# A two-block transformer in fp32 on one core: every small product widened to 128 contraction rows, and the states of the gated linear attention made for two chunks at a time

## The chip, the cores and the metric

The program runs on one core of one Trainium2 chip. The metric is the device time of one execution in microseconds, the median of three runs. The trace comes from one more execution, taken by the hardware profiler. TensorE (PE in the rows) does the matrix products, VectorE (DVE) and ScalarE (ACT) work on rows of 128 partitions, GpSimd (POOL) does memsets and a few additions, SyncE (SP) issues the transfers. An operand of TensorE has its contraction along the partitions: a product over 64 rows uses 64 partitions of both operands.

## The reference

512 tokens and 16 meta tokens (528 rows, 1024 features). Block 1 has two layers, each with two mixers side by side, an output projection and a convolutional feed-forward part. Block 2 has an attention in which each query sees the 256 or fewer keys that an index score picks, a short convolution, gates and a gated feed-forward part. What the change touches, cut short:

```python
# gated linear attention: 4 heads, dk 64, dv 128; chunk 0 = the 16 meta tokens, then 8 chunks of 64
u = einsum('bhntk,bhntv->bhnkv', k * exp(log_end - log_b), v)     # one state increment a chunk
S[c] = decay[c][..., None] * S[c-1] + u[c]                         # S[0] = the meta tokens' increment
o = einsum('bhntk,bhnkv->bhntv', q, S)                             # each token reads its chunk's state
# forgetting attention (FoX): 8 heads of 64, query blocks of 128
logits = einsum('bqhd,bkhd->bhqk', q, k) + c_q[..., None] - c_k;  p = softmax(where(causal, logits, -inf));  o = p @ v
# index scores of block 2: 8 heads of 64
rel = relu(einsum('bthd,bsd->bths', q_idx, k_idx));  score = einsum('bths,bth->bts', rel, w_idx)
# its attention: 8 heads of 128 over the chosen keys
```

## The kernel before

**Jobs.** Nearly all of the time goes to products of the activations with weights. A job is one block of 128 weight columns (`steps`, L291): for each 128 rows of the contraction it runs three passes, high part of the weights with the high and the low part of the activations, and low part with high (names wh and wl, L309). 528 tokens are two pieces of 264 columns, 512 without the meta tokens one piece of 512 or, in block 2, two of 258. A step of a job is thus four matmuls with wh and two with wl. Weights arrive by transfers issued ahead; ScalarE and VectorE split them into wh and wl two jobs ahead (L260, L261).

**Side work.** Everything else (gates, scores, softmax, transposes, values, states, norms) is pushed as small functions onto `self.queue` and taken off between a job's steps, `rate` functions a step (`pump`, L286). Attention units go through `push_unit`, stage by stage, each stage one unit later than the one before it: scores, then transposes of the probabilities, then values. The tile framework's list scheduler sets the final order on each engine from these calls; each engine then runs its list in order.

**PSUM.** Three pools of two tiles: "mm" for the jobs, "PS" (`self.PS`, used by scores, index scores, gates, spreads, states and outputs) and "PT" (`self.PT`, for transposes, values and norms). A tile is free again when its last reader is done.

**Products over fewer than 128 rows.** `stacked_scores` (L494) puts the high and the low part of a head's queries (64 features each) into the two row halves, and multiplies them by the key's high part, which stands in both halves (L497, 128 rows); the low part of the keys is multiplied by the high part of the queries alone (L498, 64 rows). FoX and the index scores use it; a FoX score ends with a product that adds the causal mask (L558, bf16), except in the first of the last block's two pieces. The 16 meta keys' values are products over 16 rows (L608 in FoX, as the first two of each group of values; L1120 for block 2, as the last of each block; L574 for the meta queries). `gla_states` (L686) makes a chunk's state increment from 64 tokens, for both heads of a pair, and chains it on VectorE:

```python
            nc.tensor.matmul(ps[:, 128 * b:128 * b + 128], lhsT=st["kt"][m][R0:R0 + 64, C],
                             rhs=st["gvt"][2 * m + b][R0:R0 + 64, C], start=True, stop=True)
...
            nc.vector.scalar_tensor_tensor(dst[R, :], z["cur"][R, :], st["dec"][m][R, c:c + 1],
                                           ps[R, 128 * b:128 * b + 128], op0=ALU.mult, op1=ALU.add)
```

One queued function is one chunk, so nine (`first` for the meta tokens, eight steps) for each of two pairs of heads in each layer. `gla_out` (L739) reads the states per chunk by products of 64 rows onto 64 tokens (L760), four in each of its two halves for each head. `spread` (L201), the gate products (L391), the 16x16 transposes of the meta queries (L568) and the last transposes of each mixer are small as well.

Of the kernel before, what the change touches and what calls it, by code (L numbers as in the profile page):

```python
# [36 lines left out]
class Net:  # L37
# [43 lines left out]
    # ---------------------------------------------------------------- constants  # L81
    def constants(self):
# [26 lines left out]
        self.wa = c.tile([16, 2, 256], F32, name="wa")  # L109
# [48 lines left out]
    # ---------------------------------------------------------------- small helpers  # L158
# [17 lines left out]
    def hs_of(self, src, gain, lo, t0=0, t1=L, hi=None):  # L176
        """hi and lo parts of src * gain over columns t0:t1."""
# [15 lines left out]
    def token_sums(self, acc):  # L193
        """Per-token sums over the features: [128, 5], one column a token block."""
# [6 lines left out]
    def spread(self, r):  # L201
        """[128, L] tile with r's per-token values in every partition."""
# [18 lines left out]
    def norm_at(self, first, sums, spread):  # L221
        """A phase's norm factors, made while its first two jobs run: sums late in the first, spread in the second."""
# [4 lines left out]
    # ---------------------------------------------------------------- weight jobs  # L227
# [17 lines left out]
    def split(self, jb, pin=False):  # L245
        """High and low parts of a job's weights; a packed job has both in one tile, 64 columns each."""
# [20 lines left out]
    def push_unit(self, stages):  # L267
        """Stages of one unit of side work; each stage goes one unit later than the stage before it."""
# [22 lines left out]
    def steps(self, jb):  # L291
        """One job's matrix products, a step for each 128 rows of the weights, then its evacuation."""
# [31 lines left out]
    def run(self, look=2, ahead=4):  # L324
        """The jobs in order; the first two go together, as their operand comes in bit by bit."""
# [25 lines left out]
    def v(t, toks):  # L351
        """View of a [128, L] tile that matches psv of the same tokens."""
# [8 lines left out]
    def scaled(self, ps, toks, rs, out=None, extra=None):  # L361
        """ps * rs (* extra) over the tokens, into a slot."""
# [8 lines left out]
    # ---------------------------------------------------------------- block 1 mixers  # L371
# [1262 lines left out]
```

## Time and profile before

| | before |
|---|---|
| three runs | 2447.89, 2444.22, 2442.56 us |
| median | 2444.22 us |
| span of the profiled execution | 2443.0 us |
| TensorE busy | 2411.0 us, 99% |
| VectorE, ScalarE, GpSimd busy | 1372.8 us (56%), 942.0 us (39%), 228.7 us (9%) |
| weight matmuls of L309 | 13720 of 15831 hardware passes |
| mean transfer rate | 81 GB/s |

The span of the profiled execution lies within the runs, so its rows stand for them. The duration that the trace gives for one matmul overlaps with the next one's; the distance from one start to the next is what a matmul takes on the engine, and the timeline's rows give the starts. A plain fp32 product is run as two hardware passes and stands as x2 there; transposes and the split (fp32r) products are one pass each. A shape like 64*128 ahead of the operand is rows times columns of the array.

### The profile page before, as it was taken

The numbers are of one execution on the slowest core, as the hardware profiler recorded it, in microseconds if no ns is written. First come the engines' busy times: TensorE is split into PE (matmuls) and PEld (weight loads), VectorE is DVE, ScalarE is ACT, GpSimd is POOL, SyncE is SP. The second block draws the span as 40 slices with busy tenths as digits, with TensorE's granted clock in tenths as the row PEclk, the third lists the DMA queues.
The fourth block names the chain that finished last, engine by engine and source line by source line (L and its number), as shares of the span: only waits on it lengthen the run. The fifth ranks groups of instructions, "written<-read, shape, count | busy, mean of one in ns | idle before, by whom it ended". The sixth has DMA issues, their size and how long they took to land.

```text
span 2443.0 us, 37854 instructions
## 1 busy us (share of the span) xinstructions
PE 2411.0 (99%) x15831; PEld 2154.9 (88%) x15831; DVE 1372.8 (56%) x2492; ACT 942.0 (39%) x1609; POOL 228.7 (9%) x216
## 2 busy tenths in 40 slices
PE   7999999999999999999999999999999999999998
PEld 6888999999998888999898988888898888888888
DVE  6556656555555666566464664688344544433335
ACT  6553434333345544434232443332233523222225
POOL 1010110000021101200000031110000002101012
PEclk9999999999998999999999999999999999999999
DMA  4211122232331111222323222232221132232233
GB/s 123 57 53 36 53 87 87 91 100 78 100 85 52 49 39 53 70 87 87 104 83 100 81 90 70 70 104 87 87 69 53 56 100 87 88 102 87 95 99 126
DMA packets 217074, 196.79 MB, mean 81 GB/s; under 512 B 8987, under 2 KB 214791, under 8 KB 216903
## 3 DMA queue, kind: packets, MB, share of 16 engines
q1 hardware_dynamic: 216903, 194.37, 25.7%
q8 instruction: 125, 2.05, 0.4%
q14 instruction: 46, 0.38, 0.1%
HBM read 192.26 MB, written 2.10 MB: 80 GB/s over the span
## 4 chain that ended last, share of the span: by engine, by line
PE 67%; ACT 1%; issue 1%; DVE 1%; POOL 0%; DMA 0%; POOLq 0%; ACTq 0%; SPq 0%; DVEq 0%
PE mm L309 59%; PE valuesT L1120 1%; PE foxV L608 1%; PE scoresS L1103 1%; PE foxS L498 1%; PE idx L498 1%; PE gla_statesS L709 0%; PE foxT L588 0%; PE attend_pT L459 0%; PE spreadS L210 0%; ACT wh L260 0%; PE foxS L497 0%; PE idx L497 0%; PE to_tokensT L445 0%; PE foxS L558 0%
## 5 line engine op out<-in xcount | busy, mean ns | idle before, releaser
L309 PE MATMUL mm<-g,wh 128*128 128x264 f32 (+3 forms) x9168 | 1890.1, 316 | 6.8 <-DVE g L365 4.5
L309 PEld LDWEIGHTS mm<-g,wh 128*128 128x128 f32 x9168 | 1389.5, 190 | 124.2 <-issue 9.8
L309 PE MATMUL mm<-g,wl 128*128 128x264 f32 (+3 forms) x4552 | 1161.8, 313 | 0.0
L309 PEld LDWEIGHTS mm<-g,wl 128*128 128x128 f32 x4552 | 751.3, 189 | 51.6 <-issue 0.3
L260 ACT ACTIVATE wh<-raw 128x1024 fp32r<-128x1024 f32 (+1 forms) x369 | 384.6, 1043 | 978.6 <-PE mm L309 831.2
L261 DVE TENSOR_TENSOR wl<-raw,wh 128x1024 fp32r<-128x1024 f32 (+1 forms) x369 | 444.8, 1206 | 83.1 <-ACT wh L260 58.1
L365 DVE TENSOR_TENSOR g<-mm,g 128x528 f32<-128x528 f32 (+2 forms) x228 | 158.6, 696 | 327.5 <-PE mm L309 324.2
L191 POOL TENSOR_TENSOR g<-g,g 128x528 f32<-128x528 f32 (+3 forms) x49 | 71.5, 1470 | 911.8 <-ACT g L190 911.8
L166 DVE TENSOR_TENSOR g<-g,g 128x512 fp32r<-128x512 f32 (+3 forms) x131 | 91.5, 698 | 39.9 <-ACT g L972 29.0
L997 DVE TENSOR_TENSOR g<-mm,g 128x528 f32<-128x528 f32 (+1 forms) x48 | 33.6, 700 | 118.7 <-PE mm L309 118.6
L954 ACT ACTIVATE g<-g,cv 128x528 f32<-128x528 f32 (+1 forms) x88 | 72.1, 820 | 17.6 <-DVE g L365 17.6
L166 DVE TENSOR_TENSOR g<-foxT,g 16x128 fp32r<-16x128 f32 (+2 forms) x160 | 49.8, 335 | 42.9 <-ACT g L593 35.9
L957 DVE SCALAR_TENSOR_TENSOR g<-g,cv,g 128x526 f32<-128x526 f32 (+1 forms) x88 | 66.8, 760 | 3.1
L956 DVE SCALAR_TENSOR_TENSOR g<-g,cv,g 128x527 f32<-128x527 f32 (+1 forms) x88 | 66.3, 753 | 1.8 <-ACT g L954 1.8
L1383 POOL TENSOR_TENSOR g<-g,g 128x512 f32<-128x512 f32 x22 | 38.9, 1767 | 283.1 <-ACT g L1382 283.1
L968 ACT ACTIVATE g<-g 128x528 f32<-128x528 f32 (+1 forms) x44 | 28.1, 639 | 84.0 <-DVE g L957 84.0
L174 POOL TENSOR_TENSOR sm<-sm,mhalf 128x10 f32<-128x10 f32 (+4 forms) x29 | 36.8, 1279 | 192.5 <-DVE sm L173 192.1
L563 ACT ACTIVATE g<-g,sm 128x144 f32<-128x144 f32 (+2 forms) x80 | 41.4, 517 | 21.1 <-DVE sm L559 18.3
L593 ACT ACTIVATE g<-foxT 128x256 fp32r<-128x256 f32 (+1 forms) x96 | 32.8, 342 | 42.8 <-PE foxT L588 36.8
L970 DVE TENSOR_TENSOR g<-g,g 128x528 f32<-128x528 f32 (+1 forms) x44 | 30.8, 701 | 32.3 <-ACT g L968 32.3
L972 ACT ACTIVATE g<-g 128x528 fp32r<-128x528 f32 (+1 forms) x44 | 28.1, 639 | 33.1 <-DVE g L970 33.1
L1414 DVE TENSOR_TENSOR g<-mm,g 128x512 f32<-128x512 f32 x16 | 11.1, 692 | 50.2 <-PE mm L309 50.2
(264 smaller groups left out, 1699.0 us busy)
## 6 DMA issues: line engine op xcount, KB each, us to landing
raw<-in_w_up_dram SPq DMA_DIRECT2D x50, 1024.0 KB
raw<-in_w_in_dram SPq DMA_DIRECT2D x44, 1024.0 KB
raw<-in_w_down_dram SPq DMA_DIRECT2D x28, 896.0 KB
raw<-in_w_in_dram SPq DMA_DIRECT2D x28, 512.0 KB
raw<-in_w_out_dram SPq DMA_DIRECT2D x12, 1024.0 KB
raw<-in_w_down_dram SPq DMA_DIRECT2D x12, 1024.0 KB
raw<-in_w_gate_dram SPq DMA_DIRECT2D x10, 1024.0 KB
raw<-in_w_up_dram SPq DMA_DIRECT2D x10, 512.0 KB
```

The costliest lines, as they stand in the source:

```text
L166: (eng or self.nc.vector).tensor_tensor(out, x, hi.bitcast(F32), op=ALU.subtract)
L191: nc.gpsimd.tensor_tensor(acc[:, t0:t1], tmp[:, t0:t1], acc[:, t0:t1], op=ALU.add)
L260: keep(nc.scalar.activation(hi[:, :K], src, AF.Copy))
L261: keep(nc.vector.tensor_tensor(lo[:, :K], src, hi[:, :K].bitcast(F32), op=ALU.subtract))
L309: nc.tensor.matmul(ps[:, b, :n], lhsT=w[:, k, :], rhs=x[:, t:t + n], start=(ki == 0 and pi == 0), stop=(ki == len(order) - 1 and pi == len ...
L365: self.nc.vector.tensor_tensor(self.v(out, toks), self.psv(ps, toks), self.v(rs, toks), op=ALU.mult)
L498: self.nc.tensor.matmul(ps[:, :n], lhsT=q[R, q0:q0 + 128], rhs=kl[R, a:a + n], start=False, stop=stop)
L563: nc.scalar.activation(P[:qs, :N], P[:qs, :N], AF.Exp, scale=-1.0, bias=m, accum_out=col)
L954: nc.scalar.activation(A[:, lo:], U[:, lo:], AF.Identity, bias=self.vec("cb", 44 * i + t), scale=cw(2))
L956: nc.vector.scalar_tensor_tensor(A[:, s1:], U[:, s1 - 1:L - 1], cw(1), A[:, s1:], op0=ALU.mult, op1=ALU.add)
L957: nc.vector.scalar_tensor_tensor(A[:, s0:], U[:, s0 - 2:L - 2], cw(0), A[:, s0:], op0=ALU.mult, op1=ALU.add)
L1383: nc.gpsimd.tensor_tensor(z[:, META:], z[:, META:], self.rs[:, META:], op=ALU.mult)
```

## The change

Each product over fewer than 128 rows gets 128 rows, the added ones being zero in one operand or both; and the gated linear attention is arranged so that one product covers two chunks.
- `fox_k` makes one tile of low key parts per head, with zeros in the other head's rows; `stacked_scores` uses all rows. The index keys' low part is built the same way.
- The meta values (`fvm`, `fvms`, `dvm`), the meta keys and values of the linear attention (`km`, `gvm`) and the low-rank gate weights (`wa`) become constants of 128 rows that are zeroed once at the start on GpSimd. `sm`, the gates' input, has its upper rows zeroed.
- `attend_p` transposes all of the first 128 columns of the probabilities as its first block and multiplies them with the zero-padded meta values; up to four blocks share a PSUM tile. FoX's meta columns and the tails are transposed 128x128 as well; `spread` uses all rows for the last, short block.
- `gla_k` writes the keys per head with the two chunks of a 128-token block in different columns, zeros elsewhere (a memset, one copy on ScalarE and one on VectorE), so that one product over 128 tokens gives two chunks' increments in the two row halves. `gla_states` has per pair `first` and two functions `head`, each four products into one PSUM tile and then eight chained VectorE operations that alternate between the halves; the decays are made per head (eight activations a layer in place of two).
- `gla_q`, new, spreads each head's queries over the two row halves by chunk (a memset, two copies on ScalarE, one on VectorE), and `gla_out` needs two products for each half.

```diff
-            nc.vector.tensor_scalar(dg[:sz, :sz], self.ident[:sz, :sz], r[:sz, j:j + 1], None, op0=ALU.mult)
+            nc.vector.tensor_scalar(dg[:, :sz], self.ident[:, :sz], r[:, j:j + 1], None, op0=ALU.mult)
             t, o = (tiles[0], b) if b < HALF else (tiles[1], b - HALF)
-            nc.tensor.matmul(t[:, o:o + sz], lhsT=self.ones[:sz, :], rhs=dg[:sz, :sz], start=True, stop=True)
+            nc.tensor.matmul(t[:, o:o + sz], lhsT=self.ones, rhs=dg[:, :sz], start=True, stop=True)
...
-    def attend_p(self, P, j, qs, vt, vm, mcol, vw, vc):
-        nc = self.nc
+    def attend_p(self, P, j, vt, vm):
+        nc = self.nc
+        cols = [0] + [BLK[k][0] for k in range(1, j + 1)]
+        vals = [vm] + [vt[:, 128 * k:128 * k + 128] for k in range(j)]
         blocks = []
-        if j:
+        for x in range(0, j + 1, 4):
+            n = min(4, j + 1 - x)
             pt = self.PT("attend_pT_")
-            for k in range(1, j + 1):
-                b, _ = BLK[k]
-                nc.tensor.transpose(pt[:, 128 * (k - 1):128 * (k - 1) + qs], P[:qs, b:b + 128],
-                                    self.ident[:qs, :qs])
-            PTs = self.G()
-            self.copy("a" if j % 2 else "v", PTs[:, :128 * j], pt[:, :128 * j])
-            for k in range(1, j + 1):
-                blocks.append((PTs[:, 128 * (k - 1):128 * (k - 1) + qs],
-                               vt[:, 128 * (k - 1) + vc:128 * (k - 1) + vc + vw]))
-        pm = self.PT("attend_pT_")
-        nc.tensor.transpose(pm[:META, :qs], P[:qs, :META], self.ident[:qs, :qs])
-        PM = self.M()
-        self.copy("v", PM[:META, :qs], pm[:META, :qs])
-        blocks.append((PM[:META, :qs], vm[:META, mcol:mcol + vw]))
+            for k in range(n):
+                nc.tensor.transpose(pt[:, 128 * k:128 * k + 128], P[:, cols[x + k]:cols[x + k] + 128], self.ident)
+            PTs = self.G() if n > 1 else self.M()
+            self.copy("v" if x or j % 2 else "a", PTs[:, :128 * n], pt[:, :128 * n])
+            blocks += [(PTs[:, 128 * k:128 * k + 128], vals[x + k]) for k in range(n)]
...
-        st["kl"] = kl = self.G(F32R)
+            kh, kl = self.G(F32R), self.G(F32R)
+            nc.gpsimd.memset(kl[O, :].bitcast(F32), 0.0)
...
-        self.nc.tensor.matmul(ps[:, :n], lhsT=q[R, q0:q0 + 128], rhs=kl[R, a:a + n], start=False, stop=stop)
+        self.nc.tensor.matmul(ps[:, :n], lhsT=q[:, q0:q0 + 128], rhs=kl[:, a:a + n], start=False, stop=stop)
...
+        pv = pt.rearrange("p (j b k) -> p j b k", j=4, b=2)
+        for b in range(2):
+            kt = self.G()
+            nc.gpsimd.memset(kt[:, :512], 0.0)
+            kv = kt[:, :512].rearrange("p (j e k) -> p j e k", j=4, e=2)
+            for e in range(2):
+                R = slice(64 * e, 64 * e + 64)
+                self.copy("v" if e else "a", kv[R, :, e, :], pv[R, :, b, :])
...
-        def step(c):
-            def f():
-                R0, C = 64 * (c % 2), slice(128 * (c // 2), 128 * (c // 2) + 128)
-                ps = self.PS("gla_statesS_")
-                for b in range(2):
-                    nc.tensor.matmul(ps[:, 128 * b:128 * b + 128], lhsT=st["kt"][m][R0:R0 + 64, C],
-                                     rhs=st["gvt"][2 * m + b][R0:R0 + 64, C], start=True, stop=True)
-                dst = z["S"][1 + c // 4][:, 128 * (c % 4):128 * (c % 4) + 128]
-                for b in range(2):
-                    R = slice(64 * b, 64 * b + 64)
-                    nc.vector.scalar_tensor_tensor(dst[R, :], z["cur"][R, :], st["dec"][m][R, c:c + 1],
-                                                   ps[R, 128 * b:128 * b + 128], op0=ALU.mult, op1=ALU.add)
-                z["cur"] = dst
-            return f
-        self.push(first, *[step(c) for c in range(8)])
+                S, ps = self.G(), self.PS("gla_statesS_")
+                for j in range(4):
+                    C = slice(128 * j, 128 * j + 128)
+                    nc.tensor.matmul(ps[:, C], lhsT=st["kt"][h][:, C], rhs=st["gvt"][h][:, C], start=True, stop=True)
+                cur = st["S0"][m][64:, 128 * b:128 * b + 128]
+                for c in range(8):
+                    e, C = c % 2, slice(128 * (c // 2), 128 * (c // 2) + 128)
+                    R, Q = slice(64 * e, 64 * e + 64), slice(64 - 64 * e, 128 - 64 * e)
+                    nc.vector.scalar_tensor_tensor(S[R, C], cur, st["dec"][h][Q, c // 2:c // 2 + 1], ps[R, C],
+                                                   op0=ALU.mult, op1=ALU.add)
+                    cur = S[R, C]
+                st["S"][h] = S
+            return f
+        self.push(first, head(0), head(1))
...
+    def gla_q(self, st, m, t):
+        nc = self.nc
+        for b in range(2):
+            B = slice(64 * b, 64 * b + 64)
+            q = self.G()
+            nc.gpsimd.memset(q, 0.0)
+            tv = t[:, META:].rearrange("p (j e t) -> p j e t", j=4, e=2)
+            qv = q[:, META:].rearrange("p (j e t) -> p j e t", j=4, e=2)
+            nc.scalar.activation(qv[:64, :, 0, :], tv[B, :, 0, :], AF.Copy)
+            nc.vector.tensor_copy(qv[64:, :, 1, :], tv[B, :, 1, :])
+            nc.scalar.activation(q[64:, :META], t[B, :META], AF.Copy)
+            st["gq"][2 * m + b] = q
...
-                for c in range(4 * half, 4 * half + 4):
-                    Sc = (SA if c < 4 else SB)[:, 128 * (c % 4):128 * (c % 4) + 128]
-                    t, x, s0 = META + 64 * c, 128 * (c // 2), 64 * (c % 2)
-                    nc.tensor.matmul(ps[s0:s0 + 64, x:x + 128], lhsT=gq[B, t:t + 64], rhs=Sc[B, :],
+                for j in (2 * half, 2 * half + 1):
+                    C = slice(128 * j, 128 * j + 128)
+                    nc.tensor.matmul(ps[:, C], lhsT=gq[:, META + 128 * j:META + 128 * j + 128], rhs=S[:, C],
                                      start=True, stop=True)
```

Where the instructions stand: on TensorE, in the first layer behind the transposes of a pair's keys and values, before (gla_statesS is the PSUM tile of a chunk's increments, mm a job's):

```order
L309 MATMUL mm_2417<-g_205,wl_2066 128x264 x2
L445 MATMUL to_tokensT_2391<-ident,g_2209 128x128 x4
L448 MATMUL to_tokensT_2397<-ident,g_2209 16x128
L709 MATMUL gla_statesS_2438<-g_1734,g_569 128x128
L709 MATMUL gla_statesS_2438<-g_1744,g_569 128x128
L309 MATMUL mm_2417<-g_223,wh_2065 128x264 x2
L309 MATMUL mm_2417<-g_224,wh_2065 128x264 x2
L309 MATMUL mm_2417<-g_223,wl_2066 128x264 x2
L709 MATMUL gla_statesS_2449<-g_1734,g_569 128x128
L709 MATMUL gla_statesS_2449<-g_1744,g_569 128x128
```

and now:

```order
L322 MATMUL mm_2460<-g_226,wl_2106 128x264
L463 MATMUL to_tokensT_2431<-ident,g_2249 128x128 x4
L466 MATMUL to_tokensT_2437<-ident,g_2249 16x128
L322 MATMUL mm_2460<-g_226,wl_2106 128x264
L735 MATMUL gla_statesS_2479<-g_1774,g_602 128x128 x4
L322 MATMUL mm_2460<-g_244,wh_2105 128x264 x2
L322 MATMUL mm_2460<-g_245,wh_2105 128x264 x2
L322 MATMUL mm_2460<-g_244,wl_2106 128x264 x2
L735 MATMUL gla_statesS_2499<-g_1784,g_606 128x128 x4
L322 MATMUL mm_2460<-g_264,wh_2105 128x264 x2
```

Where a chunk's two products stood in every step of the job, a head's four stand together, two heads one step apart, each group in a PSUM tile of its own.

On VectorE the recurrence of the same pair, before (s is the start state, g a slot of states, dec the decays; each row is both heads):

```order
L714 SCALAR_TENSOR_TENSOR g_2430<-s_2424,dec_557,gla_statesS_2438 64x128 x2
L166 TENSOR_TENSOR g_2402<-g_2400,g_2407 64x528
L714 SCALAR_TENSOR_TENSOR g_2430<-g_2430,dec_557,gla_statesS_2449 64x128 x2
L714 SCALAR_TENSOR_TENSOR g_2430<-g_2430,dec_557,gla_statesS_2454 64x128 x2
L714 SCALAR_TENSOR_TENSOR g_2430<-g_2430,dec_557,gla_statesS_2465 64x128 x2
L714 SCALAR_TENSOR_TENSOR g_2431<-g_2430,dec_557,gla_statesS_2476 64x128 x2
```

and now:

```order
L740 SCALAR_TENSOR_TENSOR g_2478<-s_2467,dec_577,gla_statesS_2479 64x128
L740 SCALAR_TENSOR_TENSOR g_2478<-g_2478,dec_577,gla_statesS_2479 64x128
L179 TENSOR_TENSOR g_2449<-g_2440,g_2448 64x528
L740 SCALAR_TENSOR_TENSOR g_2478<-g_2478,dec_577,gla_statesS_2479 64x128
L740 SCALAR_TENSOR_TENSOR g_2498<-s_2467,dec_580,gla_statesS_2499 64x128
L740 SCALAR_TENSOR_TENSOR g_2478<-g_2478,dec_577,gla_statesS_2479 64x128
L740 SCALAR_TENSOR_TENSOR g_2498<-g_2498,dec_580,gla_statesS_2499 64x128
L740 SCALAR_TENSOR_TENSOR g_2478<-g_2478,dec_577,gla_statesS_2479 64x128
```

Each chunk had a PSUM tile of its own, released after two operations; now eight operations read one tile, and the two heads' chains alternate.

On TensorE the first FoX units of the first layer, before (foxS are scores, foxT transposes, foxV values):

```order
L558 MATMUL foxS_855<-maskb,identb 128x16
L309 MATMUL mm_781<-g_269,wh_659 128x264 x2
L309 MATMUL mm_781<-g_270,wh_659 128x264
L568 MATMUL foxT_861<-ident,g_839 16x16
L309 MATMUL mm_781<-g_270,wh_659 128x264
L309 MATMUL mm_781<-g_269,wl_660 128x264 x2
L574 MATMUL foxV_867<-vm_801,md_863 16x64
L497 MATMUL foxS_878<-g_651,g_714 128x256
```

and now:

```order
L570 MATMUL foxS_895<-maskb,identb 128x128
L322 MATMUL mm_824<-g_288,wh_702 128x264 x2
L322 MATMUL mm_824<-g_289,wh_702 128x264 x2
L322 MATMUL mm_824<-g_288,wl_703 128x264
L580 MATMUL foxT_901<-ident,g_879 128x128
L322 MATMUL mm_824<-g_288,wl_703 128x264
L510 MATMUL foxS_918<-g_690,g_757 128x256
L511 MATMUL foxS_918<-g_691,g_757 128x256
L570 LDWEIGHTS identb
L570 MATMUL foxS_918<-maskb,identb 128x128
```

The meta queries' transposes and values keep their place between the weight matmuls, and have 128 rows.

## Rows read from the trace of the kernel before

**Rows 1.** The page's busy times of the engines

```profile
PE 2411.0 (99%) x15831; PEld 2154.9 (88%) x15831; DVE 1372.8 (56%) x2492; ACT 942.0 (39%) x1609; POOL 228.7 (9%) x216
```

**Rows 2.** Mixer stretch: us; busy PE, PEld, DVE, ACT, POOL; clock; DMA share, GB/s

```profile
56.00:292.00 236.00, 235.87 (x1705) 202.63 (x1703) 147.08 (x394) 116.14 (x293) 29.17 (x45) 1.00 0.17 50
```

**Rows 3.** Waits of TensorE: total us, times, longest us

```profile
PE to_tokensT L445 <- DVE g L676: 3.6, 1, 3.6
```

**Rows 4.** Timeline of TensorE, index scores: start us, us, instruction

```profile
1504.90 0.64 PE L309 MATMUL mm<-g,wh 128*128 128x258 f32 x4
1505.38 0.40 PE L309 MATMUL mm<-g,wl 128*128 128x258 f32 x2
1505.62 0.34 PE L497 MATMUL idx<-g,g 128*128 128x400 f32 x1
1505.90 0.44 PE L498 MATMUL idx<-g,g 64*128 64x400 f32 x1
1506.27 0.76 PE L309 MATMUL mm<-g,wh 128*128 128x258 f32 x4
```

**Rows 5.** Timeline of TensorE, attention of block 2

```profile
1781.69 1.05 PE L1120 MATMUL valuesT<-g,g 128*128 128x128 f32 x8
1782.68 0.48 PE L1120 MATMUL valuesT<-md,dvm 16*128 16x128 f32 x2
1783.09 0.75 PE L309 MATMUL mm<-g,wh 128*128 128x264 f32 x4
1783.68 0.40 PE L309 MATMUL mm<-g,wl 128*128 128x264 f32 x2
```

**Rows 6.** Timeline of TensorE, states of the gated linear attention

```profile
195.56 0.41 PE L309 MATMUL mm<-g,wl 128*128 128x264 f32 x2
195.90 0.71 PE L709 MATMUL gla_statesS<-g,g 64*128 64x128 f32 x4
196.54 0.74 PE L309 MATMUL mm<-g,wh 128*128 128x264 f32 x4
```

**Rows 7.** Timeline of TensorE, FoX scores; a 16x16 transpose behind a mask

```profile
79.23 0.28 PE L497 MATMUL foxS<-g,g 128*128 128x256 f32 x1
...
79.75 0.23 PE L558 MATMUL foxS<-maskb,identb 128*128 128x128 bf16 x1
79.79 0.72 PE L309 MATMUL mm<-g,wh 128*128 128x264 f32 x4
80.35 0.41 PE L309 MATMUL mm<-g,wl 128*128 128x264 f32 x2
...
163.97 0.23 PE L558 MATMUL foxS<-maskb,identb 128*128 128x128 bf16 x1
164.13 0.18 PE L568 MATMUL foxT<-ident,g 16*16 16x16 f32 x1
164.24 0.76 PE L309 MATMUL mm<-g,wh 128*128 128x264 f32 x4
164.84 0.28 PE L309 MATMUL mm<-g,wl 128*128 128x264 f32 x1
```

**Rows 8.** Timeline of TensorE, outputs of the gated linear attention

```profile
264.54 0.39 PE L753 MATMUL gla_outT<-s,g 64*16 64x128 f32 x2
264.86 0.65 PE L760 MATMUL gla_outS<-g,g 64*64 64x128 f32 x8
265.44 0.76 PE L309 MATMUL mm<-g,wh 128*128 128x264 f32 x4
```

**Rows 9.** Transposes by line and shape: count, busy us, mean ns, idle

```profile
L588 PE MATMUL foxT<-ident,g 128*128 128x128 f32 x160 | 28.4, 274 | 0.0
...
L596 PE MATMUL foxT<-ident,g 128*16 128x128 f32 x64 | 17.6, 275 | 0.0
```

**Rows 10.** VectorE's recurrence by line: count, busy us, mean ns, idle

```profile
L714 DVE SCALAR_TENSOR_TENSOR g<-g,dec,gla_statesS 64x128 f32<-64x128 f32 x56 | 19.4, 347 | 11.5 <-PE gla_statesS L709 10.5
```

**Rows 11.** GpSimd's memsets by line

```profile
L524 POOL MEMSET o<- 128x128 f32 x8 | 1.6, 211 | 180.2 <-DVE sm L649 177.4 <-PE foxN L669 2.7
```

More of the change, by code (lines that the diff above doesn't have):

```diff
@@ L108, in constants @@
         self.bf = c.tile([40, 2], F32, name="bf")
-        self.wa = c.tile([16, 2, 256], F32, name="wa")
+        self.km, self.gvm = c.tile([128, 512], F32, name="km"), c.tile([128, 512], F32, name="gvm")
+        nc.gpsimd.memset(self.km, 0.0)
+        nc.gpsimd.memset(self.gvm, 0.0)
+        self.wa = c.tile([128, 2, 256], F32, name="wa")
+        nc.gpsimd.memset(self.wa, 0.0)
+        self.fvm, self.fvms, self.dvm = [], [], []
+        for x in range(2):
+            self.fvm.append(c.tile([128, 128], F32, name=f"fvm{x}"))
+            self.fvms.append([c.tile([128, 128], F32R, name=f"fvms{x}{b}") for b in range(2)])
+            self.dvm.append(c.tile([128, 128], F32, name=f"dvm{x}"))
+            for t in (self.fvm[x], self.fvms[x][0], self.fvms[x][1], self.dvm[x]):
+                nc.gpsimd.memset(t.bitcast(F32), 0.0)
     def vectors(self):
@@ L515, in fox_prep @@
         nc.tensor.transpose(pm[:META, :128], st["fv"][:, :META], self.ident)
[L516 to L518 removed]
+        st["vm"], st["vms"] = self.fvm[p % 2], self.fvms[p % 2]
+        nc.vector.tensor_copy(st["vm"][:META], pm[:META, :128])
         for b in range(2):
             C = slice(64 * b, 64 * b + 64)
[L521 to L522 removed]
+            nc.scalar.activation(st["vms"][b][:META, :64], pm[:META, C], AF.Copy)
+            self.lo_sub(st["vms"][b][:META, 64:], pm[:META, C], st["vms"][b][:META, :64])
         st["O"] = self.opool.tile([128, 5, 128], F32, tag="o", name=self.n("o"))
@@ L544, in fox_unit @@
         r = 64 * b
-        q0, qs = BLK[j]
+        q0, qs = BLK[j] if j else (0, 128)
         N = q0 + qs
@@ L573, in trans_meta @@
             o = self.PT("foxV_")
-            nc.tensor.matmul(o[:META, :64], lhsT=PM[:META, :META], rhs=st["vm"][:, r:r + 64], start=True, stop=True)
+            nc.tensor.matmul(o[:, :64], lhsT=PM, rhs=st["vm"][:, r:r + 64], start=True, stop=True)
             nc.vector.tensor_scalar(st["O"][:META, 0, r:r + 64], o[:META, :64], rc[:META, 0:1], None, op0=ALU.mult)
@@ new lines, in first, with head, f @@
+                nc.tensor.matmul(ps[:, 128 * b:128 * b + 128], lhsT=self.km[:, C], rhs=self.gvm[:, C],
+                                 start=True, stop=True)
+            nc.vector.tensor_copy(S0, ps[:, :256])
+            st["S0"][m] = S0
+        def head(b):
+            def f():
+                h = 2 * m + b
+                S, ps = self.G(), self.PS("gla_statesS_")
+                for j in range(4):
+                    C = slice(128 * j, 128 * j + 128)
[8 more added lines that the diff above has]
+                st["S"][h] = S
@@ L737, in head_norm @@
         return scale
+    def gla_q(self, st, m, t):
+        nc = self.nc
+        for b in range(2):
+            B = slice(64 * b, 64 * b + 64)
[7 more added lines that the diff above has]
+            st["gq"][2 * m + b] = q
     def gla_out(self, st, m):
@@ L815, in spread @@
             self.rs = self.spread(nr["r"])
-        def start():
-            st["km"] = self.meta.tile([META, 256], F32, tag="km", name=self.n("km"))
-            st["gvm"] = self.meta.tile([META, 512], F32, tag="gvm", name=self.n("gvm"))
         def ev_sm(ps):
@@ L826, in ev_sm @@
             nc.vector.tensor_tensor(sm[R, :], t[R, :], self.rs[R, :], op=ALU.mult)
+            nc.gpsimd.memset(sm[64:, :], 0.0)
             self.push(*self.gates(i, sm, st))
@@ L830, in layer @@
         first = len(self.jobs)
-        self.job(c_sm, 0, hs, FULL, ev_sm, side=[start])
+        self.job(c_sm, 0, hs, FULL, ev_sm)
         self.jobs[-1]["packed"] = True
@@ L1290, in prep @@
                     d["vt"] = self.G()
-                    d["vm"] = self.meta.tile([META, 128], F32, tag="dvm", bufs=2, name=self.n("dvm"))
+                    d["vm"] = self.dvm[h % 2]
                     self.to_tokens(d["v"], d["vt"], d["vm"], 0, "a")
```

92 lines of the change are left out of this document (43 added, 49 removed).

## The prediction

> **What bounds the kernel now.** I read the page's busy times first, then a table by stage, then the waits of TensorE. TensorE is busy 2411.0 us of the 2443.0 us span [rows 1], so only some 32 us are idle; the wait for the gate chain in front of the first token transposes is 3.6 of them [rows 3]. In the first mixer stretch TensorE is at 235.87 of 236 us while VectorE has 147.08 and ScalarE 116.14; the granted clock is 1.00 there, the 2.4 GHz level [rows 2]. A busy TensorE isn't yet one that streams columns: what counts is what a side matmul costs between two weight matmuls, and that is read from start to start in the timeline. There the reader is to see what a matmul costs that contracts over fewer rows than the one ahead of it and the one behind it.
>
> **The price of one excursion.** In the index scores the weight matmuls of 258 columns start 0.12 us apart (four in 0.48, two in 0.24) [rows 4]. By columns a 400-wide one is worth 0.186. The pair that follows takes 0.28 for its first matmul, which still has 128 rows, and 0.37 for the second, which has 64: 0.09 and 0.18 too much. In the attention eight plain value matmuls take 0.99, the two passes of the 16-row one 0.41, and the four weight matmuls behind it 0.59 where four usually take 0.48 [rows 5]. With 0.10 of the 0.99 put down to the coming switch, a plain pass is worth 0.111, so that the 16-row pair carries 0.19 too much and the matmuls behind it 0.10. In the states of the gated linear attention the two weight matmuls ahead take 0.34 instead of 0.24, and the four passes of 64 rows 0.64 where 4 x 0.111 is 0.44 [rows 6]. All three places say the same: about 0.10 going in, 0.19 coming out, 0.10 on the next matmuls, **0.385 us** for each excursion from 128 rows, no matter if it has 16 or 64 rows, one format or the other.
>
> The Trainium skill has a rule that speaks against this change: "TensorE: Matmul & The Clock Gate", section "Why this matters for your kernels", says that a single matmul over 32 rows takes as long as one over 128, and that what small ones gain comes from running beside each other in the array. By that rule widening saves nothing but whole passes, about 12 us in all, and the time would be 2431 instead of 2340. No row above agrees with it once a small matmul stands between wide ones, since it misses the switch on either side.
>
> **What the widening takes away.** Counts are from the loops; order shows that the widened instructions keep their places.
> - Index scores: 8 heads x 5 pieces = 40 x 0.385 = 15.4 us.
> - FoX scores: 2 layers x 8 heads x 6 pieces = 96. In 16 nothing covers the way out: 6.2. In 80 the mask's bf16 matmul stands behind. That pair from start to the end of the next four weight matmuls takes 1.12 [rows 7]; clean it is 2 x 0.119 (256 columns) + 0.49 and the mask, for which the traces have no clean row: 0.04 (what it shows here) to 0.12 (a 264-column weight matmul). That leaves 0.27 to 0.35; I take 0.31, with the mask at 0.08. 80 x 0.31 = 24.8; together 31.0.
> - FoX values against the meta rows: 32 pairs x 0.385 = 12.3. Values of block 2 against the meta rows: 8 heads x 4 blocks = 32 x 0.385 = 12.3.
> - States: 2 layers x 2 x 9 steps = 36 x 0.385 = 13.9. Besides, 144 hardware passes become 80: 64 x 0.111 = 7.1.
> - Outputs of the gated linear attention: before, the meta product's two passes and eight passes of 64x64 take 0.32 + 0.58 [rows 8], with 0.10 each for the ways in and out 1.10; after, there are six full passes, 0.67. That is 0.43 for each of 8 first halves. The second halves lack the 0.32: 0.78 against 0.44. Together 6.1; where two heads stand side by side they share the way in and out, so I take 5. The 64x64 passes do run close together (0.07 apart), and still lose, because two chunks in one product need half as many.
> - Small ones: the 16x16 transposes (16) cost 0.16 - 0.04 on the mask ahead and 0.60 - 0.49 on the matmuls behind [rows 7]: 0.23 each, 3.7. For the 16 meta values of FoX and the 16 tail transposes I take 0.23 and for the gate products (8) 0.2: 9.0. The 7 spreads at 0.385: 2.7. Together 15.4; all these at nothing would lose 9.0 of it, all at 0.385 would add some 9.
>
> Sum: 15.4 + 31.0 + 12.3 + 12.3 + 13.9 + 7.1 + 5 + 15.4 = **112 us**. The 96 transposes that use 16 columns of the array get 128 now; one takes 275 ns at 16 and 274 at 128 columns [rows 9], so I take nothing; if the wider weights cost even half of a plain pass more, 96 x 0.056 = 5 us would come on top, which the range holds. The 24 evacuations that the joined meta block saves on VectorE lie beside other work.
>
> **What it adds.** Memsets on GpSimd: 45, the largest 512 to 528 columns. The trace has 128 columns at 211 ns [rows 11]; by columns at most 0.87 each, about 30 us in all on an engine busy 29.17 of 236 us in a mixer stretch [rows 2]. They are first in their tiles and wait for nothing but a free slot: hidden by that idle time, bound 0 to 30 if each stood ahead of its reader with nothing beside it; I take 0. Six more decay activations a layer, and the 16 FoX units of the meta queries at 128 columns in place of 16, fall into the half of ScalarE's and VectorE's time that is free [rows 2]. The low-rank weights' load now waits for their memset at the start; nothing else is on GpSimd then and its reader comes some 20 us later: 0.
>
> The recurrence: eight steps of VectorE at 347 ns [rows 10] now hang behind four matmuls in one PSUM tile, 2.8 us, and the two heads' chains interleave on VectorE, 5.6 us, with both tiles of that pool held. By order the next user of the pool stands 36 weight matmuls behind the second head, 4.4 us, plus the two heads' own passes of 0.9 each; VectorE also has an operation of another kind among them. So TensorE would wait 0 to 2 us there. Behind the second pair the next score stands some 10 us away: nothing. I take 2 us a layer, 4 in all; below nothing isn't to be had, since TensorE didn't wait here before. Queued behind a waiting matmul are all weight matmuls.
>
> The padded queries (a memset, two copies on ScalarE, one on VectorE per head) come between the query's evacuation and its first output product: about 1 us more latency, and side work closer together by a sixth in the mixers, where VectorE goes from 62% to some 75% of a stretch that shrinks from 236 to about 195 us. For the waits that come from that I take 4 more, 2 to 20 for both. The gate chain's 3.6 stays.
>
> 2443.0 - 112 + 8 = 2339 for the profiled execution. The median of the runs is 2444.2, 1.2 above the span; I say **2340**, and 2322 to 2364 for this case alone (stalls 2 to 20, mask and small ones at their ends).
>
> **The rivals.**
> - *The mixers become bound by latency.* With 0.385 less at each side step, TensorE reaches the scores, transposes and values before VectorE and ScalarE have their inputs. For: 82 of the 112 us fall in the two mixer stretches, and each unit is a chain over three engines. Against: TensorE idles 0.13 us in 236 now, and VectorE has 89 free. If half of the 82 is lost, 2340 + 41 = 2381; if less than a quarter, it is still the first case.
> - *More than the sum.* Each excursion that I discounted (80 masked, 56 small) costs the full 0.385, and no new wait comes: 15 more won and 8 fewer lost, 2317.
> - *The change doesn't take away what it is made for.* What I read as the price of fewer rows is that of another operand, or of plain against reduced fp32, and stays. Against: the eight plain value matmuls of 128 rows, with other operands and another format than the weight matmuls around them, run at 0.11 each [rows 5]. Only passes are saved: 2443 - 12 = 2431. The skill's rule ends here too.
> - *Slower.* As the one before, and the eight chains of 2.8 us lie open, each before the next user of its PSUM tile: 2431 + 22 = 2453. It decides from the point at which the chains expose more than the widening saves, so it needs a saving under 22 us. Against: the distance of 4.4 us and more in order.
>
> **Numbers.** First case 0.68, latency 0.17, more 0.06, only passes 0.05, slower 0.04. The range from 2315 to 2382 takes in the first, most of the second and third: 0.84 of it by these chances, and I leave it so because the stalls are the least known term. 0.2% is about what a measurement of this kernel can tell from no change. Faster by more than that: 0.95; within: 0.01; slower: 0.04.
>
> **What would show it.** In the profile after: the weight matmuls 0.12 apart directly behind a score, a value product or a state, and no 0.59 for four; 0.25 for an index pair of 272; mixer stretches of 195 to 200 us each, the index stretch shorter by 15, the attention by 12; TensorE idle under 45 us in all. Wrong it would be if TensorE waits for VectorE's recurrence or for scaled queries by tens of us, if the granted clock falls under 1.00 in the mixers, or if the gap behind a score stays with 128 rows.

## The result, and the profile after

The changed kernel takes 2360.61 us, median of four runs (2358.55 to 2361.31), against 2443.39 for the kernel before on the same chip: a ratio of 0.9657, 95% interval 0.9643 to 0.9671, 82.8 us less. The forecast was 2340, the range 2315 to 2382.

The page's first line, with busy time, share and instructions of each engine, and TensorE's longest waits (total us, times, longest us), with the one for an evacuation in the kernel before as the last row:

```profile
PE 2318.5 (98%) x15703; PEld 2133.4 (90%) x15703; DVE 1378.4 (58%) x2480; ACT 952.2 (40%) x1641; POOL 248.3 (11%) x261
```
```profile
PE mm L322 <- DVE g L378: 11.7, 3, 4.8
PE to_tokensT L694 <- DVE g L690: 3.8, 1, 3.8
```
```profile
PE mm L309 <- DVE g L365: 4.5, 1, 4.5
```

TensorE's busy time is down by 92.5 us [rows 1], its idle time up from 32 to 41. The gate chain's wait is what it was [rows 3]. New are two waits of 3.49 us for VectorE's line 378; their row holds a third, of 4.8 us at the start of layer 2, which the kernel before had too (4.5 us).

The places of rows 4 to 6 now. First the index scores, then the values of block 2's attention (start us, us, instruction):

```profile
1446.06 0.65 PE L322 MATMUL mm<-g,wh 128*128 128x258 f32 x4
1446.54 0.40 PE L322 MATMUL mm<-g,wl 128*128 128x258 f32 x2
1446.78 0.34 PE L510 MATMUL idx<-g,g 128*128 128x400 f32 x1
1446.96 0.35 PE L511 MATMUL idx<-g,g 128*128 128x400 f32 x1
1447.15 0.64 PE L322 MATMUL mm<-g,wh 128*128 128x258 f32 x4
1447.63 0.40 PE L322 MATMUL mm<-g,wl 128*128 128x258 f32 x2
```
```profile
1704.42 0.39 PE L1158 MATMUL valuesT<-g,dvm 128*128 128x128 f32 x2
1704.64 0.83 PE L1158 MATMUL valuesT<-g,g 128*128 128x128 f32 x6
1705.23 0.73 PE L322 MATMUL mm<-g,wh 128*128 128x264 f32 x4
1705.80 0.40 PE L322 MATMUL mm<-g,wl 128*128 128x264 f32 x2
```

The pair of 400 columns takes 0.18 + 0.19 in place of 0.28 + 0.37 [rows 4], and the four weight matmuls behind it 0.48. In the attention, eight passes and four weight matmuls take 1.38 from 1704.42 to 1705.80, and 8 x 0.111 + 0.48 is 1.37. The four behind it still stand at 0.57, which I had said would go: here the passes ahead are shorter by as much (six in 0.59). Behind a plain product 0.1 moves from one row to the next, and only the sum from clean start to clean start can be read.

The first mixer stretch, from the same place to the start of the output job, then ten-microsecond windows around its end (window, its us, busy PE, PEld, DVE, ACT, POOL, clock, DMA share, GB/s):

```profile
56.00:267.00 211.00, 206.45 (x1636) 197.01 (x1636) 150.81 (x399) 118.38 (x302) 35.14 (x59) 0.98 0.19 56
```
```profile
240.00:250.00 10.00, 10.00 (x85) 9.96 (x85) 9.75 (x23) 7.17 (x16) 7.89 (x8) 1.00 0.01 2
250.00:260.00 10.00, 6.51 (x50) 6.33 (x48) 7.68 (x13) 3.49 (x5) 0.00 (x0) 0.90 0.30 106
260.00:270.00 10.00, 10.00 (x67) 10.00 (x67) 4.27 (x8) 2.75 (x4) 0.00 (x0) 0.76 0.01 2
```

236 us have become 211, not the 195 to 200 that I gave as a sign. At 250 to 260 TensorE is idle for 3.5 us, and its granted clock is down in that window and the next, 0.90 and 0.76: in part of them it runs at the 1.2 GHz level. So one of my signs of being wrong, a clock under 1.00 in the mixers, has come (0.98 in the stretch). What TensorE waits for is seen on TensorE, VectorE and ScalarE there:

```profile
254.78 0.40 PE L322 MATMUL mm<-g,wl 128*128 128x264 f32 x2
258.67 1.22 PE L322 MATMUL mm<-g,wh 128*128 128x264 f32 x4 [3.49 <-DVE g L378]
259.69 0.65 PE L322 MATMUL mm<-g,wl 128*128 128x264 f32 x2
```
```profile
254.42 0.89 DVE L829 SCALAR_TENSOR_TENSOR g<-gla_tailT,cv,g 128x272 f32<-128x272 f32 x2
256.06 1.22 DVE L274 TENSOR_TENSOR wl<-raw,wh 128x1024 fp32r<-128x1024 f32 x1 [0.75 <-ACT wh L273]
257.21 0.70 DVE L179 TENSOR_TENSOR g<-g,g 128x528 fp32r<-128x528 f32 x1
257.82 1.32 DVE L378 TENSOR_TENSOR g<-mm,g 128x528 f32<-128x528 f32 x2
```
```profile
254.97 1.06 ACT L273 ACTIVATE wh<-raw 128x1024 fp32r<-128x1024 f32 x1 [2.75 <-PE mm L322]
255.94 0.63 ACT L830 ACTIVATE g<-g 128x528 fp32r<-128x528 f32 x1
```

The next weight matmul needs a PSUM tile that VectorE's evacuation (L378) has to free. In VectorE's list that stands behind the second head's tail (L829, L179) and the split of a later job's weights (L274). The split waits for ScalarE's half of it, which starts at 254.97, when TensorE has given a weight buffer back. So TensorE waits for work that itself waited for TensorE's progress. In the kernel before, one split stands between two evacuations at this place in VectorE's list; now there are three. From the orders of the two kernels, before and now, with other rows left out:

```
L365 TENSOR_TENSOR g_3329<-mm_3157,g_362 128x528
...
L261 TENSOR_TENSOR wl_3438<-raw_2952,wh_3437 128x1024
L166 TENSOR_TENSOR g_3403<-g_3404,g_3402 128x528
L365 TENSOR_TENSOR g_3434<-mm_3338,g_362 128x528
```
```
L378 TENSOR_TENSOR g_3343<-mm_3187,g_381 128x528
...
L274 TENSOR_TENSOR wl_3349<-raw_2982,wh_3348 128x1024
...
L274 TENSOR_TENSOR wl_3452<-raw_2982,wh_3451 128x1024
...
L274 TENSOR_TENSOR wl_3510<-raw_3346,wh_3509 128x1024
L179 TENSOR_TENSOR g_3417<-g_3418,g_3416 128x528
L378 TENSOR_TENSOR g_3448<-mm_3352,g_381 128x528
```

Two corrections to the section on the change. The index keys' low part stood in both row halves before as well; there only the rows used have grown, and the product now holds low times low too. And not every small product has 128 rows now: the 32 products of FoX's key gates (foxC) keep 72, and show no excursion:

```profile
69.85 0.40 PE L548 MATMUL foxC<-c,sel 72*128 72x272 bf16 x2
70.01 0.73 PE L322 MATMUL mm<-g,wh 128*128 128x264 f32 x4
```

Two of them and the four weight matmuls behind (the next row starts at 70.58) take 0.73, which is six times 0.12.

### The profile page after: what moved, and what is told of

It is laid out like the page before. It is cut to its first block, busy times and chain, and to the rows that moved or that the text cites. A ratio compares the mean times of both kernels' runs of the same rounds, so it can differ in the third digit from the quotient of the medians.

```text
span 2359.5 us, 37628 instructions
## 1 busy us (share of the span) xinstructions
PE 2318.5 (98%) x15703; PEld 2133.4 (90%) x15703; DVE 1378.4 (58%) x2480; ACT 952.2 (40%) x1641; POOL 248.3 (11%) x261
## 4 chain that ended last, share of the span: by engine, by line
PE 66%; ACT 1%; DVE 1%; issue 1%; POOL 0%; DMA 0%; POOLq 0%; ACTq 0%; SPq 0%
PE mm L322 59%; PE valuesT L1158 1%; PE scoresS L1141 1%; PE foxV L620 1%; PE attend_pT L480 1%; PE foxT L600 0%; ACT wh L273 0%; PE foxS L510 0%; POOL g L204 0%; PE spreadS L223 0%; PE foxS L511 0%; PE idx L510 0%; DMA raw<-in_w_down_dram 0%; PE to_tokensT L463 0%; PE idx L511 0%
## 5 line engine op out<-in xcount | busy, mean ns | idle before, releaser
L274 DVE TENSOR_TENSOR wl<-raw,wh 128x1024 fp32r<-128x1024 f32 (+1 forms) x369 | 445.1, 1206 | 66.0 <-ACT wh L273 55.8
L378 DVE TENSOR_TENSOR g<-mm,g 128x528 f32<-128x528 f32 (+2 forms) x228 | 158.5, 696 | 318.7 <-PE mm L322 315.4
L179 DVE TENSOR_TENSOR g<-g,g 128x512 fp32r<-128x512 f32 (+3 forms) x131 | 92.1, 703 | 38.2 <-ACT g L1010 29.0
L179 DVE TENSOR_TENSOR g<-foxT,g 128x128 fp32r<-128x128 f32 (+1 forms) x160 | 50.5, 340 | 20.3 <-ACT g L605 18.0
L187 POOL TENSOR_TENSOR sm<-sm,mhalf 128x10 f32<-128x10 f32 (+3 forms) x29 | 37.2, 1290 | 115.2 <-DVE sm L186 114.9
```

The lines of the kernel that those rows point to most:

```text
L179: (eng or self.nc.vector).tensor_tensor(out, x, hi.bitcast(F32), op=ALU.subtract)
L187: self.nc.gpsimd.tensor_tensor(out, v[:rows, :n], self.mhalf[:rows, :n], op=ALU.pow)
L274: keep(nc.vector.tensor_tensor(lo[:, :K], src, hi[:, :K].bitcast(F32), op=ALU.subtract))
L378: self.nc.vector.tensor_tensor(self.v(out, toks), self.psv(ps, toks), self.v(rs, toks), op=ALU.mult)
```

## The experiments

Each ran against the kernel before on its own chip; times are medians, intervals 95%. Two theories stand behind them: that the prices of the prediction are right and waits in the mixers took back the rest, or that the prices or counts were too high.

The medians carry some 3 us of uncertainty by their intervals. A stretch can be read more closely: the trace of each run has all 13720 weight matmuls, and in nearly the same order, so a stretch is taken here from one of them, counted from the start, to another. In us:

| run | first mixer, 227th to 1224th | index scores, 9049th to 9607th | attention, 10682nd to 11547th |
|---|---|---|---|
| before | 230.1 | 104.9 | 209.7 |
| block 2 alone | 230.1 | 89.4 | 196.5 |
| FoX's scores alone | 216.4 | 104.8 | 209.3 |
| FoX's meta rows alone | 222.4 | 104.8 | 209.1 |
| linear attention alone | 223.5 | 104.9 | 209.2 |
| the same, ends mended | 217.8 | 104.8 | 209.4 |
| changed | 205.3 | 89.4 | 196.1 |
| changed, 96 rows | 203.6 | 89.5 | 196.0 |
| changed, 64 rows | 205.1 | 97.0 | 196.0 |
| changed, memsets twice | 203.3 | 89.4 | 196.4 |
| changed, ends mended | 198.2 | 89.3 | 196.4 |

Runs with the same kernel code in a stretch of block 2 agree on it within 0.6 us. In the first mixer the changed kernel's form spreads from 203.3 to 205.3, by the low clock behind the wait at its end: from 255 to 270 the granted clock is 0.77 in the changed kernel and 0.89 in the run with the memsets twice.

**Block 2 alone.** The kernel before, with the rows of the index scores' low products and the attention's first block as in the change:

```diff
-        R = slice(64 * b, 64 * b + 64)
+        R = slice(0, 128) if b is None else slice(64 * b, 64 * b + 64)
...
-                self.stacked_scores(ps, qi[h], box["kh"], box["kl"], h % 2, q0, a, max(n, 256), True)
+                self.stacked_scores(ps, qi[h], box["kh"], box["kl"], None, q0, a, max(n, 256), True)
```

> The kernel before with the widening in block 2 alone: index scores over 128 rows (40 excursions fewer) and the meta values of its attention over 128 rows (32 fewer); both mixers as before. Theory 1 (the prices of the prediction are right, and waits in the mixers took back the rest): there are no mixers in it, so the full 72 x 0.385 = 27.7 us come, 25 to 29 us under before. Theory 2 (the price was read too high, 0.385 is about 0.29): 19 to 22 us under before. In the trace, theory 1 shows the weight matmuls behind an index pair 0.12 us apart and no idle time that before doesn't have.

2417.61 against 2443.91: 26.3 us less (ratio 0.9893, 0.9878 to 0.9907). The price of 0.385 holds where no mixer is: 0.365 for each of the 72 by the medians. In the traces the index scores are 15.5 us shorter (40 of them, 0.39 each; forecast 15.4) and the attention 13.2 (32, 0.41 each; forecast 12.3).

**96 rows and 64 rows.** The changed kernel, with the low product of the four even index heads cut to the first 96, or 64, rows:

```diff
-        self.nc.tensor.matmul(ps[:, :n], lhsT=q[:, q0:q0 + 128], rhs=kl[:, a:a + n], start=False, stop=stop)
+        self.nc.tensor.matmul(ps[:, :n], lhsT=q[:rows, q0:q0 + 128], rhs=kl[:rows, a:a + n], start=False, stop=stop)
...
-                self.stacked_scores(ps, qi[h], box["kh"], box["kl"], q0, a, max(n, 256), True)
+                self.stacked_scores(ps, qi[h], box["kh"], box["kl"], q0, a, max(n, 256), True, 128 if h % 2 else 96)
```

> The changed kernel with the low products of the even index heads over 96 rows in place of 128 (20 matmuls; they leave out the low part of the queries' lower half with the low part of the keys, rows 96 to 127). If any count of rows other than the neighbours' is an excursion: 20 x 0.385 = 7.7 us over the changed kernel, with 0.28 and 0.37 for a pair of 400 columns. If 96 rows are run like 128: no difference within 2 us, and pairs at 0.18 a matmul.

> The changed kernel with the low products of the even index heads over 64 rows, as before the change (20 matmuls; the odd heads keep 128). The counterpart of the run with 96 rows. By the price of an excursion: 20 x 0.385 = 7.7 us over the changed kernel, 6 to 9. If the price were that of something else than the row count: within 2 us of it.

96 rows: 2360.49, no different from the changed kernel's 2360.61. 64 rows: 2368.53, 7.9 us more (ratio to before 0.9695, 0.9681 to 0.9708, against 0.9657), which is 20 x 0.395. In the traces the index stretch takes 89.5 us with 96 rows and 97.0 with 64, against 89.4: 7.6 more, 20 x 0.38. A pair of the one and of the other, with a weight matmul group behind:

```profile
1444.85 0.35 PE L510 MATMUL idx<-g,g 128*128 128x400 f32 x1
1445.04 0.35 PE L511 MATMUL idx<-g,g 96*128 96x400 f32 x1
1445.22 0.65 PE L322 MATMUL mm<-g,wh 128*128 128x258 f32 x4
```
```profile
1446.56 0.34 PE L510 MATMUL idx<-g,g 128*128 128x400 f32 x1
1446.83 0.45 PE L511 MATMUL idx<-g,g 64*128 64x400 f32 x1
1447.21 0.75 PE L322 MATMUL mm<-g,wh 128*128 128x258 f32 x4
1447.79 0.41 PE L322 MATMUL mm<-g,wl 128*128 128x258 f32 x2
```

At 96 rows the matmuls are 0.19 and 0.18 apart, at 64 they show 0.27 and 0.38, and 0.58 for the four behind. Same tiles, same place, same format: the price is that of the 64 rows, and not of every count other than 128. This settles the rival by which the change doesn't take away what it is made for.

**FoX's scores alone.** The kernel before with `fox_k` and the scores' low products as in the change.

> The kernel before with FoX's scores alone over 128 rows (a tile of low key parts per head with zeros from GpSimd); all else as before. The prediction's term is 31.0 us. In the changed kernel's trace a masked pair costs as much as if the mask took 0.12, the upper bound, which makes it 80 x 0.27 + 6.2 = 28. Theory A (term right but for the mask): 26 to 31 us under before. Theory B (the units then wait for ScalarE and VectorE, in waits too short to show as idle time): 17 to 24 us.

2415.96 against 2443.12: 27.2 us less (0.9888, 0.9875 to 0.9902). Theory A; the first mixer is 13.7 us shorter. The mask's clean price, which no row of before had, is in the changed kernel:

```profile
103.33 0.28 PE L511 MATMUL foxS<-g,g 128*128 128x256 f32 x1
103.45 0.23 PE L570 MATMUL foxS<-maskb,identb 128*128 128x128 bf16 x1
103.50 0.72 PE L322 MATMUL mm<-g,wh 128*128 128x264 f32 x4
104.06 0.41 PE L322 MATMUL mm<-g,wl 128*128 128x264 f32 x2
```

From 103.45 to 104.06 the mask and four weight matmuls take 0.61; the four are 0.49, so the mask is 0.12, my upper bound.

**FoX's meta rows alone.** The kernel before with its meta values, meta queries and tail transposes at 128 rows.

> The kernel before with FoX's meta rows alone widened: values against the meta rows (32 pairs), meta queries' transposes and values (16 and 16), the meta columns' transposes and the 8 of the tail. The prediction's terms: 12.3 + 3.7 + 3.7 + 1.8 = 21.5 us. Theory A: 18 to 22 us under before. Theory B (short waits and excursions that stand side by side and share their ways in and out): 9 to 15 us.

2426.50 against 2443.12: 16.6 us less (0.9928, 0.9914 to 0.9942), between the two theories. One of the 16 small value products, before (two passes of 16 rows) and in this run:

```profile
114.07 0.28 PE L309 MATMUL mm<-g,wl 128*128 128x264 f32 x1
114.28 0.28 PE L574 MATMUL foxV<-vm,md 16*16 16x64 f32 x2
114.49 0.39 PE L309 MATMUL mm<-g,wl 128*128 128x264 f32 x1
114.72 0.49 PE L642 MATMUL foxN<-ident,g 128*128 128x128 f32 x3
```
```profile
112.24 0.40 PE L315 MATMUL mm<-g,wl 128*128 128x264 f32 x2
112.60 0.41 PE L579 MATMUL foxV<-fvm,md 128*128 128x64 f32 x2
112.84 0.61 PE L647 MATMUL foxN<-ident,g 128*128 128x128 f32 x4
```

Two weight matmuls and the pair took 0.65 and take 0.60. The pair itself takes 0.24, no less than one of 128 columns, where the small one took 0.21, and the weight matmul ahead of it takes 0.24. This one gains 0.05; I had put 0.23 on each. It isn't typical of the 16: in others of this run the pair takes 0.14,

```profile
158.34 0.33 PE L579 MATMUL foxV<-fvm,md 128*128 128x64 f32 x2
158.48 0.48 PE L613 MATMUL foxV<-g,fvms 128*128 128x256 f32 x2
```

and what it adds between its neighbours, 0.40 to 0.41 before, is 0.21 to 0.39 now, some 0.3 on the mean: a gain of 0.1.

The larger term, the 32 pairs of FoX values, falls short as well. Measured from the start of the matmul ahead to the start of the fourth pass, the 26 that stand by themselves take 0.18 to 0.40 less than before, 0.33 on the mean against 0.385; in those that gain least, the matmul ahead or the first pass still takes 0.2 or more. The other six stand directly behind one of the small pairs, and the two together gain 0.28 on the mean, where I had put 0.385 + 0.23. The first mixer is 7.7 us shorter.

**The linear attention alone, and its ends mended.** The kernel before with `gla_k`, `gla_states`, `gla_q`, `gla_out` and its tails as in the change; then the same with the first two heads' tails out of the side queue:

```diff
                 if h == 0:
-                    self.push(tail, *st["scale"][1])
-                elif h == 1:
-                    self.push(tail)
-                else:
-                    first_out["at"] = {**first_out.get("at", {}), 2 * h - 2: [tail]}
+                    self.push(*st["scale"][1])
+                first_out["at"] = {**first_out.get("at", {}), (0, 1, 2, 4)[h]: [tail]}
```

> The kernel before with the gated linear attention alone in its new form (states of two chunks in one product, padded queries, outputs, its tail transposes); FoX, gates, spreads and block 2 as before. By the prediction's prices it removes 13.9 + 7.1 + 5 + some 2 = 28 us of TensorE's time. Theory 1: the mixers stay longer by the FoX part, so VectorE keeps up, and 22 to 28 us show. Theory 1b (the new wait at the end of each mixer belongs to the new form itself, its padded queries and late norms): 14 to 20 us under before, with a wait of about 3.5 us of TensorE for VectorE's evacuation at the end of each mixer. Theory 2 (price too high): 17 to 21 without such a wait.

> The kernel of the run with the linear attention alone, and the first two heads' tails in the first steps of the output job, as in the run that mends the end of the mixers. If that run's shortfall of 14 us against 28 is the wait at the ends (2 x 3.5) and what the clock loses behind it: 7 to 11 us under that run, 21 to 25 under before. Rival (the terms of the linear attention are too high): within 3 us of that run.

Alone: 2429.70, 14.2 us less (0.9944, 0.9928 to 0.9961), with the wait:

```profile
PE mm L312 <- DVE g L368: 11.5, 3, 4.5
```

Mended: 2422.66, 20.5 us less (0.9913, 0.9899 to 0.9926), with one wait of that kind left, of 4.5 us, as before the change; just under the 21 to 25 that I expected. So the two waits belong to the linear attention's new form, and cost 7.0 us here. The first mixer is 12.3 us shorter with its end mended.

**The changed kernel with its ends mended.** The same edit in the changed kernel.

> The changed kernel with the first two heads' tails of the gated linear attention taken out of the side queue and put into the first two steps of the first output job, beside the other two heads' tails, so that VectorE's evacuations of the gate jobs don't stand behind them. Theory 1: the 3.49 us waits for an evacuation at the end of both mixers go or shrink below 1 us each, and with them the half-clock stretch behind the first: 5 to 11 us faster than the changed kernel. Rival: the tails are then late for the output job's steps 4 and 5 and TensorE waits there instead: within 3 us of the changed kernel.

2352.00, ratio 0.9624 (0.9609 to 0.9638): 8.6 us under the changed kernel, 91.9 under before, the fastest of all. Its waits, the window and the mean clock of each (the changed kernel's first):

```profile
PE mm L322 <- DVE g L378: 4.7, 1, 4.7
```
```profile
250.00:260.00 10.00, 10.00 (x84) 9.88 (x83) 7.36 (x13) 2.99 (x5) 0.18 (x1) 1.00 0.34 107
260.00:270.00 10.00, 10.00 (x84) 9.98 (x83) 7.41 (x12) 5.72 (x8) 0.00 (x0) 1.00 0.13 34
```
```profile
core 0: 2359.5 us, clock 0.992
```
```profile
core 0: 2350.8 us, clock 0.995
```

Both waits of 3.49 us are gone, and with them the low clock behind the first, which is why the first mixer is 7.1 us shorter, twice the wait. VectorE's list has one split between two evacuations there again, and VectorE waits for TensorE:

```profile
248.63 0.70 DVE L378 TENSOR_TENSOR g<-mm,g 128x528 f32<-128x528 f32 x1
251.24 1.22 DVE L274 TENSOR_TENSOR wl<-raw,wh 128x1024 fp32r<-128x1024 f32 x1
253.68 0.71 DVE L378 TENSOR_TENSOR g<-mm,g 128x528 f32<-128x528 f32 x1 [1.22 <-PE mm L322]
```

**The same edit in the kernel before,** as control.

> The kernel before with nothing but the first two heads' tails moved into the output job's first steps, as control for the run that mends the end of the mixers. If the wait there is the change's own doing: within 2 us of before, since TensorE has no wait there. If the tails' place costs something in any case: 4 to 9 us faster than before.

2445.14 against 2444.99 (1.0001, 0.9992 to 1.0010): nothing. The tails' place costs only with the linear attention's new form.

**Memsets twice.** The changed kernel with the 32 memsets of low keys, keys and queries issued twice.

> The changed kernel with each of the 32 memsets of the low key parts, the keys and the queries issued twice (16.6 us more on GpSimd, at the 525 to 539 ns that they take in the changed kernel's trace). The prediction took them at nothing: within 3 us of the changed kernel. Rival (they stand ahead of their readers with nothing beside them): up to 17 us slower, with the mixers' stretches longer by 8 each.

2364.62, ratio 0.9673 (0.9657 to 0.9689) against 0.9657 (0.9643 to 0.9671): 1 us outside what I expected, with intervals that overlap, so by times alone it is open. The traces settle the rival: the first mixer takes 203.3 us here and 205.3 in the changed kernel, the second, taken in the same way from the 4926th to the 6065th weight matmul, 219.1 and 219.4; neither is longer by 8. In its trace GpSimd has 21 us more (269.5), TensorE's busy time is 2319.4 against 2318.5, and its idle time is 3.5 us longer, 2.1 of that in waits for the first loads, in front of which no memset of these stands, and 1.5 in one more wait at the gate chain. Whether that one is the memsets' doing is open.

## Why the prediction was right, by its steps

The forecast of 2340 was 20.6 us too low; the range held, and so did the 2322 to 2364 of the first case alone, near its slow end. The price behind it was right, and the sum was too high.

| term | forecast us | measured alone us |
|---|---|---|
| index scores and values of block 2 | 15.4 + 12.3 | 26.3 |
| FoX scores | 31.0 | 27.2 |
| FoX meta values and small ones | 12.3 + 9.2 | 16.6 |
| linear attention: states, outputs, tails | 27.8 | 20.5, with its ends mended |
| spreads and gates | 4.3 | not run alone |
| sum | 112 | 90.6 without the last |
| new waits | -8 | -8.6, by mending the ends |

- **The price of one excursion** was right where the excursion stands alone: 0.365 over 72 and 0.395 over 20 by the medians, 0.39, 0.41 and 0.38 in the stretches of the traces. It goes away in full with 96 or 128 rows, and the gate products show none with 72. The Trainium skill's rule on single small matmuls ("TensorE: Matmul & The Clock Gate", "Why this matters for your kernels") differs from what the runs with these 72 and 20 show at 64 rows, and the measurement decides; a 32-row one, of which the rule speaks, no run here has.
- **The sum of the terms** is the step that was off, 112 where the parts give 91 and the whole with its ends mended 91.9. All that is missing is missing in the mixers: the index scores and the attention gave what was forecast. I had put 82 us on the two mixers, 41 on each; the first gains 31.9 with its ends mended, and the parts alone 13.7, 7.7 and 12.3, together 33.7. The spreads and gates are in the whole and not in the parts, so that either they gain nothing or the parts take a few us from each other; no run tells these apart. Some of the 20 us is sized: the mask at its upper bound (80 x 0.04, 3.2), and FoX's products with the meta values, where 26 pairs at 0.33, six at 0.28 together with the small one ahead of them, and ten small ones at 0.1 make some 11 us of the forecast 16. What is missing in the linear attention's terms isn't settled.
- **The new waits** had the right size by luck, for the wrong reason. I put 4 us on the recurrence, with both PSUM tiles held; TensorE doesn't wait for it once (no such row among its waits). The 4 for the closer spacing of the side work were too little: 7.0 us of idle time at the two ends, and some clock behind it, which the mended kernel gets back as 8.6. That is close to the rival that I called latency, a late VectorE, at the mixers' ends alone and at a fifth of its price.
- **The memsets** at nothing held in the mixers, by the stretches of the run with twice as many. 528 columns take 534 to 539 ns, not the 0.87 us that columns in proportion gave.
- The rival "slower" needed a saving under 22 us and open chains: neither came.

## What to carry to other kernels

Where narrow products stand singly between wide ones on a busy TensorE, what they cost is the change to 64 or 16 rows and back, some 0.38 us each in this kernel, less where they stand side by side or in front of a short product; padding the contraction with zeros to the neighbours' size removes it, and the zeros can come from an idle engine. Price it from clean start to clean start, the way in and the next matmuls included, and compare two kernels from the same weight matmul to the same one. And when the saved time shortens a stretch, look at what stands ahead of the next evacuation in the other engines' lists: one that came in time before came 3.5 us late here, and moving two functions gave a tenth of the whole gain on top.

## What the runs showed that I had not expected

- A product over 96 rows runs among 128-row ones as if it had 128; at 64 rows it costs 0.38 us more. The 72-row products of the gates show no cost either.
- A plain fp32 pair with 128 rows and 64 columns takes 0.14 to 0.24, at worst no less than one of 128 columns.
- A wait of 3.49 us on a TensorE that had been busy throughout was followed by matmuls at half rate (weight matmuls 0.22 to 0.26 apart from 258.67 to 261, granted clock 0.76 in the window from 260). The wait of 3.49 us in the second layer was not; the four behind it take 0.56 to the next row, at 939.55:

```profile
938.99 0.72 PE L322 MATMUL mm<-g,wh 128*128 128x258 f32 x4 [3.49 <-DVE g L378]
```

- A run's time goes with its mean granted clock: the 13 runs of the kernel before beside the last two experiments take 2442.2 to 2445.0 us at 0.995 or 0.996, and 2445.3 to 2448.3 at 0.993 or 0.994. That is as much as one of the smaller terms, so that the difference between the two profiles above (0.992 and 0.995) can't be put down to the waits alone.
